# Splitting the input norm's product of x, gain and power into two products, on one core

## The chip, the cores and the metric

The kernel runs on 1 core of one Trainium2 chip. The metric is the device time of one execution in microseconds (us), the median of several runs. Engines are called by their short names: PE (matrix products; PEld is its weight load), DVE (vector), ACT (scalar activations), POOL (GpSimd), SP (the engine whose queue issues the DMAs here).

## The reference

Two layers over x of 256 tokens by 1024 features, float32. Each layer has three sublayers, every one between an input norm and an output norm:

```
def rms_norm(x, g):
    xf = x.astype(jnp.float32)
    y = xf * lax.rsqrt(jnp.mean(xf * xf, axis=-1, keepdims=True) + EPS)
    return (y * g.astype(jnp.float32)).astype(x.dtype)
...
    for l in range(DEPTH):
        h = swiglu(rms_norm(x, ffn1_pre[l]), ffn1_w_gate_up[l], ffn1_w_down[l])
        x = x + 0.5 * rms_norm(h, ffn1_post[l])
        h = hybrid_mixer(rms_norm(x, mix_pre[l]), w_in[l], b_gate[l], conv_w[l],
                         w_conv_out[l], w_pool_group[l], b_pool_group[l],
                         pool_scale[l], w_pool_out[l], w_o[l])
        x = x + rms_norm(h, mix_post[l])
        h = swiglu(rms_norm(x, ffn2_pre[l]), ffn2_w_gate_up[l], ffn2_w_down[l])
        x = x + 0.5 * rms_norm(h, ffn2_post[l])
    return x
```

The mean over features, its power of -0.5 and the gain vector g make the factor; the change concerns `rms_norm` where it stands ahead of a sublayer. There are six of those (two layers of three sublayers).

## The kernel before, in words

Tokens are cut into two blocks of 128 (`NB`, L22), and x stays on the chip as `xs[b]`, 128 tokens by 1024 features. Weights come in chunks of 1 MB through the SP queue; `issue` (L108) loads each in two halves `raw`, ACT copies a rounded high part `hi`, DVE takes the rest `lo`. Every product is made of high and low parts, so PE has three products where the reference has one.

A sublayer ends with `out_product` (L270): it finishes block 0's output first, then calls `on_block(0, ...)` and goes on with the last 12 steps (three matmuls each) of block 1. `on_block` (L524) calls `post` (L216), which adds the normed output to x, and then `pre` (L234), which makes the next sublayer's input `xn`. `turn` (L245) transposes a half of `xn` on PE and splits it into `xt`, which the next sublayer reads. The two halves of block 0 are turned after steps 8 and 10 of those 12 (`TURN0`, L35). Block 1 goes through the same functions after its last step; its halves are turned inside `fill` (L311), the next sublayer's first products, after 5 and 6 half products of block 0 (`TURN1`, L33).

`pre` takes two sums of squares on ACT (`sumsq`, L210, tile `junk`, result `ss`), and then `rstd` (L200): two DVE instructions `v` on one column, the second reading the first's result, and the power `r` on POOL (L207). In block 1 a part of a weight's split (`lo`) stands on DVE between the update of x and `pre` (the `part()` at the end of `post`).

Ahead of the first sublayer the trunk loads x block 0, the gain vector, x block 1 and then weights, all through SP in this order, and runs `pre` and `turn` for block 0; `r` of block 1 is made early, and `pre(1, g0, r)` gets it as an argument. PE has 13 warming matmuls in the meantime.

The order of the instructions on PE, ACT and DVE is the order of the program: `InOrder` (L43) keeps it, and in the profile all these instructions bear its line, L49. The tiles' names tell them apart.

Of the kernel before, what the change touches and what calls it, by code (L numbers as in the profile page):

```python
# [10 lines left out]
F32 = mybir.dt.float32  # L11
# [3 lines left out]
ALU = mybir.AluOpType  # L15

P = 128
T = 256
D = 1024
# [16 lines left out]

# Columns of the per-feature parameters: gate bias, conv taps, pool bias, pool scale.
F_BG, F_CW, F_PB, F_PS, F_N = 0, 16, 40, 48, 56


class InOrder:
    """An engine whose instructions are kept in the order of the program."""

# [9 lines left out]
def trunk(ctx: ExitStack, tc: tile.TileContext, x, gains, feat, wgu1, wd1, win, wco, wpg, wpo, wo, wgu2, wd2, out):  # L53
    nc = tc.nc
# [17 lines left out]

# [1 line left out]
    xs = [const.tile([P, D], F32, name=f"x{b}") for b in range(NB)]  # L74

    def load_x(b):
        for h in HALF:
            nc.sync.dma_start(xs[b][:, h], x[b * P : (b + 1) * P, h])  # L78

    ident = const.tile([P, P], F32, name="ident")  # L80
    make_identity(nc, ident)
    mhalf = const.tile([P, 1], F32, name="mhalf")
    nc.gpsimd.memset(mhalf, -0.5)
    invc = const.tile([P, PAD], F32, name="invc")
    for i in range(PAD):
        nc.gpsimd.memset(invc[:, i : i + 1], 1.0 / (i + 1))

# [1 line left out]
    stream = []  # L89
# [18 lines left out]
    def issue(now=True):  # L108
        """Loads and splits the next chunk, or leaves the parts of the split for part()."""
        i = state["issued"]  # L110
        state["issued"] = i + 1
        name, l, c = stream[i]
        hi = whi.tile([P, CHUNK], F32R, name="hi")
        lo = wlo.tile([P, CHUNK], F32R, name="lo")
        h = CHUNK // 2
        for s in range(2):
            sl = slice(s * h, (s + 1) * h)
            raw = raws.tile([P, h], F32, name="raw")
            nc.sync.dma_start(raw, src[name][l, c, :, sl])
            parts.append(lambda sl=sl, raw=raw: act.copy(hi[:, sl], raw))  # L120
            parts.append(
                lambda sl=sl, raw=raw: dve.tensor_tensor(lo[:, sl], raw, hi[:, sl].bitcast(F32), op=ALU.subtract)
            )
        ready[i] = (hi, lo)
        if now:
            part(4)
# [8 lines left out]
    def chunk(name, held=0):  # L135
        """The next chunk; held: how many of the chunks before it are still to be read."""
        i = state["used"]
        assert stream[i][0] == name, (stream[i], name)
        state["used"] = i + 1
        top_up(held + 1)  # L140
        if state["issued"] == i + 1:
            part(len(parts))
        return ready.pop(i)

    def top_up(held):
        """Loads and splits ahead, into the buffers that are not held; held chunks are still to be
        read. The last split is left to part()."""
        part(len(parts))
        while state["issued"] < min(state["used"] + LOOK + 1 - held, len(stream)):
            part(len(parts))  # L150
            issue(False)

# [1 line left out]
    def split(dst, src_ap, between=0):  # L154
        """dst = (high, low) views; src in PSUM or SBUF, float32."""
        hi, lo = dst
        act.copy(hi, src_ap)
        part(between)
        dve.tensor_tensor(lo, src_ap, hi.bitcast(F32), op=ALU.subtract)

    def feat_product(name, acts_hl):
        """W^T @ act for the two 128-column tiles of a chunk, features on partitions. In each of the
        two banks: the high weights with the high and with the low part of act side by side, and the
        low weights with the high part on top of the first."""
        ps = [bank(), bank()]
        whi_, wlo_ = (t.rearrange("p (k c) -> p k c", c=CC) for t in chunk(name))
        for i in range(2):
            cs = slice(i * P, (i + 1) * P)
            for k in range(KT):
                both, ah, _ = acts_hl[k]  # L170
                pe.matmul(ps[i], whi_[:, k, cs], both, start=(k == 0), stop=False)
                pe.matmul(ps[i][:, :T], wlo_[:, k, cs], ah, start=False, stop=(k == KT - 1))
        return ps

    def add_up(ps, tag, out=None):
        """The two halves of a feature product, added: [128, 2, 256]."""
        t = tmp.tile([P, 2, T], F32, name=tag)
        out = t if out is None else out
        for i in range(2):
            act.copy(t[:, i, :], ps[i][:, T:])  # L180
        part()
        for i in range(2):
            dve.tensor_tensor(out[:, i, :], ps[i][:, :T], t[:, i, :], op=ALU.add)
        return out

    def token_product(o, w, acts_hl, b, ks):
        """o[128 tokens of block b, 256] = act^T @ W chunk."""
        whi_, wlo_ = (t.rearrange("p (k c) -> p k c", c=CC) for t in w)
# [4 lines left out]

# [1 line left out]
    def load_gain(l, which):  # L195
# [4 lines left out]
    def rstd(parts, scale):  # L200
        """(scale * (sum of parts / D + eps)) ** -0.5"""
        v0 = small.tile([P, 1], F32, name="v0")
# [13 lines left out]
    def post(b, banks, gain, scale):  # L216
        """x[b] += rms(h) * gain / sqrt(scale)"""
        u = wide.tile([P, D], F32, name="u")
# [15 lines left out]
    def pre(b, gain, r=None):  # L234
        """rms(x[b]) * gain"""
        if r is None:
            r = rstd([sumsq(xs[b][:, HALF[s]]) for s in range(2)], 1.0)
        xn = wide.tile([P, D], F32, name="xn")
        for s in range(2):
            dve.scalar_tensor_tensor(  # L240
                xn[:, HALF[s]], xs[b][:, HALF[s]], r, gain[s], op0=ALU.mult, op1=ALU.mult
            )
        return xn

    def turn(b, s):  # L245
        """Half of the next sublayer's input of block b, features on partitions, split."""
        xn, xt = state["xn"][b], state["next"][0]
# [11 lines left out]
    def act_slot(dtype=F32):  # L259
        """[128, 2, 512] float32, or twice that in bfloat16"""  # L260
        return acts.tile([P, 2, 512], dtype, name="act", tag="act")

    def split_pair(src_ap):
        """Two feature tiles [128, 2, 256] -> (high and low side by side, high, low) of each"""
        t = act_slot(F32R).rearrange("p i (h t) -> p i h t", h=2)
        split((t[:, :, 0, :], t[:, :, 1, :]), src_ap, 1)
        return [(t[:, i], t[:, i, 0, :], t[:, i, 1, :]) for i in range(2)]

# [1 line left out]
    def out_product(name, nchunk, acts_hl, on_block):  # L270
# [40 lines left out]
    def fill(name, n, turns, acts_hl, take):  # L311
        """n chunks' products, tokens on partitions. Block 0 goes ahead, and after turns[s] halves of
        a product the s-th half of block 1's input is turned. take(b, f, ps) reads the columns of
        one or two chunks, the f-th the last."""
        ws = [chunk(name, LOOK) for _ in range(n)]
# [16 lines left out]

# [1 line left out]
    def turn_back(tok):  # L334
        """[128 tokens, 2, 256 features] of both blocks, as [128 features, 2, 256 tokens] in PSUM."""
        pt = bank()
# [5 lines left out]
    def ffn(l, gu, dn, acts_hl, on_block, nfill, turns, gains_):  # L342
        # The first nfill chunks: gate and up of a pair by turns, and a last gate.
        slot = act_slot()
# [31 lines left out]
    def mixer(l, acts_hl, on_block, nfill, turns, gains_):  # L376
# [3 lines left out]

        # Gates of the conv branch, the first of block 0 ahead of block 1.
        slots = [act_slot() for _ in range(2)]
# [22 lines left out]

        # Gated short convolution.
        ys = []
# [17 lines left out]

        # Pooling over trailing windows.
        ds_ = []
# [21 lines left out]

        # Gates of the pool branch.  # L450
        gp = gates()
# [30 lines left out]

# [1 line left out]
    plan = []  # L484
    for l in range(DEPTH):
        plan += [("ffn", l, "gu1", "d1", 0, 1, 4.0), ("mix", l, None, None, 2, 3, 1.0), ("ffn", l, "gu2", "d2", 4, 5, 4.0)]

    # The tensor engine's clock rises only after some time of work.
    idle = act_slot(BF16)[:, 0, :]
# [54 lines left out]
def _cols(w):  # L544
    """[L, 1024, N] -> [L, N / 256, 128, 8 * 256]: chunks of 256 columns, partitions first."""
    l, k, n = w.shape
# [4 lines left out]
def _rows(w):  # L551
    """[L, K, 1024] -> [L, K / 256, 128, 2 * 1024]: chunks of two row tiles, partitions first."""
    l, k, n = w.shape
# [4 lines left out]
def _gate_up(w):  # L558
    """Chunks of gate columns and of up columns by turns."""
    c = _cols(w)  # L560
# [35 lines left out]
```

## Time and profile before

| | |
|---|---|
| median of 3 runs | 1187.08 us (1185.7 to 1188.16) |
| profiled execution, span from first to last instruction | 1184.7 us |
| PE busy | 1169.6 us (99%) |
| DVE busy | 804.2 us (68%) |
| ACT busy | 639.1 us (54%) |
| POOL busy | 17.2 us (1%) |
| DMA | 225.57 MB, mean 190 GB/s |

For the profiled execution the profile gives the span; a time of its own, with what lies around the span, is not among the numbers shown. Busy time of an engine is the sum of its instructions' times; PE's is modelled, and says where PE had work, not how fast. The rows that bear on the change are below, in groups.

### The profile page before, as it was taken

Reading aid. Unit: us, or ns where it says so; the run is one execution under the profiler, and the core shown is the slowest. Engines: PE = TensorE matmul, PEld = TensorE weight load, DVE = VectorE, ACT = ScalarE, POOL = GpSimd, SP = SyncE. Lnnn points to the kernel's source line nnn. Section 1 sums busy time; section 2 is a strip of 40 time slices with the busy share of each in tenths; the row PEclk is TensorE's granted clock in tenths of the full one; section 3 lists DMA queues with packets and bytes.
Section 4 is the critical chain, followed back from the end, with each engine's and each line's share of the span. In section 5 each row is a group of like instructions: output and inputs, shape, how many; then the busy total and the mean of one; then the engine's idle time right before and its main releaser. Section 6 shows DMA issues by size and latency. Waiting matters only on the chain.

```text
span 1184.7 us, 17127 instructions
## 1 busy us (share of the span) xinstructions
PE 1169.6 (99%) x6625; PEld 1023.1 (86%) x6625; DVE 804.2 (68%) x1092; ACT 639.1 (54%) x997; POOL 17.2 (1%) x75
## 2 busy tenths in 40 slices
PE   7999999999999999999999999999999999999997
PEld 6888888988888898888898888898888888988886
DVE  5776745677987776665476666466789786766742
ACT  5755634655564565554365555356556565655630
POOL 0000000000000000000000000000000000000000
PEclk8999999999999999999999999999999999999999
DMA  7765663655566465667456566536565554756540
GB/s 267 265 188 192 194 228 132 222 184 179 171 202 209 163 230 183 196 190 231 161 193 192 185 195 230 189 128 215 182 204 185 198 181 141 243 184 194 190 167 36
DMA packets 62577, 225.57 MB, mean 190 GB/s; under 512 B 7200, under 2 KB 7200, under 8 KB 62496
## 3 DMA queue, kind: packets, MB, share of 16 engines
q1 hardware_dynamic: 62496, 224.48, 57.5%
q8 instruction: 52, 0.85, 0.3%
q14 instruction: 29, 0.24, 0.1%
HBM read 223.40 MB, written 1.05 MB: 189 GB/s over the span
## 4 chain that ended last, share of the span: by engine, by line
PE 96%; ACT 1%; DVE 1%; DMA 1%; POOL 0%; issue 0%; SPq 0%; DVEq 0%; POOLq 0%; ACTq 0%
PE ps L49 96%; ACT junk L49 1%; DMA x<-in_x 1%; POOL r L207 0%; DVE x L49 0%; DVE xn L49 0%; DVE v L49 0%; DVE lo L49 0%; ACT xt L49 0%; ACT hi L49 0%; SPq L78 0%; DVEq L592 0%; POOLq L592 0%; SPq L197 0%; ACTq L49 0%
## 5 line engine op out<-in xcount | busy, mean ns | idle before, releaser
L49 PE MATMUL ps<-xt,hi 128*128 128x512 f32 x1920 | 667.3, 392 | 0.0
L49 DVE TENSOR_TENSOR lo<-raw,hi 128x1024 fp32r<-128x1024 f32 x412 | 495.0, 1221 | 134.5 <-ACT hi L49 133.5
L49 PE MATMUL ps<-xt,lo 128*128 128x256 f32 x1920 | 537.7, 280 | 0.0
L49 ACT CAST hi<-raw 128x1024 fp32r<-128x1024 f32 x412 | 424.9, 1050 | 103.1 <-PE ps L49 89.1
L49 PEld LDWEIGHTS ps<-xt,hi 128*128 128x128 f32 x1920 | 359.2, 187 | 78.7
L49 PEld LDWEIGHTS ps<-xt,lo 128*128 128x128 f32 x1920 | 362.9, 189 | 0.1
L49 PE MATMUL ps<-hi,act 128*128 128x512 f32 x832 | 260.0, 390 | 0.0
L49 PEld LDWEIGHTS ps<-hi,act 128*128 128x128 f32 x832 | 156.2, 188 | 32.3
L49 PE MATMUL ps<-lo,act 128*128 128x512 f32 x416 | 161.9, 389 | 0.0
L49 ACT COPY h<-ps 128x256 f32<-128x256 f32 x150 | 54.5, 374 | 142.9 <-PE ps L49 141.6
L49 DVE TENSOR_TENSOR h<-ps,h 128x256 f32<-128x256 f32 x150 | 61.6, 420 | 91.7 <-ACT h L49 91.7
L49 ACT COPY sil<-ps 128x256 f32<-128x256 f32 (+1 forms) x126 | 46.7, 374 | 103.5 <-PE ps L49 103.5
L49 PE MATMUL ps<-act,hi 128*128 128x512 f32 (+1 forms) x320 | 102.0, 375 | 0.0
L49 PEld LDWEIGHTS ps<-lo,act 128*128 128x128 f32 x416 | 78.1, 188 | 15.7
L49 PE MATMUL ps<-act,lo 128*128 128x256 f32 x288 | 81.0, 281 | 0.0
L49 DVE TENSOR_TENSOR sil<-ps,sil 128x256 f32<-128x256 f32 x106 | 43.7, 420 | 49.1 <-ACT sil L49 49.1
L49 PE MATMUL ps<-hi,xt 128*128 128x256 f32 x512 | 74.4, 289 | 0.8 <-ACT hi L49 0.8
L49 ACT CAST act<-h 128x512 fp32r<-128x512 f32 x65 | 40.4, 621 | 60.9 <-DVE h L49 60.9
L49 PEld LDWEIGHTS ps<-hi,xt 128*128 128x128 f32 x512 | 67.7, 196 | 1.6 <-ACT hi L49 1.2
L49 PEld LDWEIGHTS ps<-act,hi 128*128 128x128 f32 x320 | 58.1, 189 | 12.0
L49 PEld LDWEIGHTS ps<-act,lo 128*128 128x128 f32 x288 | 54.5, 189 | 0.0
L49 DVE TENSOR_TENSOR act<-h,act 128x512 fp32r<-128x512 f32 (+1 forms) x73 | 50.1, 686 | 6.0 <-ACT act L49 5.7
(57 smaller groups left out, 450.2 us busy)
## 6 DMA issues: line engine op xcount, KB each, us to landing
raw<-in_wgu SPq DMA_DIRECT2D x176, 512.0 KB, 4.6
raw<-in_win SPq DMA_DIRECT2D x96, 512.0 KB, 4.7
raw<-in_wd SPq DMA_DIRECT2D x88, 512.0 KB, 4.6
raw<-in_wco SPq DMA_DIRECT2D x16, 512.0 KB, 5.2
raw<-in_wpo SPq DMA_DIRECT2D x16, 512.0 KB, 4.2
raw<-in_wo SPq DMA_DIRECT2D x16, 512.0 KB, 4.4
gain<-in_gains SPq DMA_DIRECT2D x12, 512.0 KB, 4.6
raw<-in_wpg SPq DMA_DIRECT2D x4, 512.0 KB, 4.2
```

The costliest lines, as they stand in the source:

```text
L49: return lambda *a, **kw: self.tc.keep_in_program_order(f(*a, **kw))
```

## The change

`pre` multiplied x by the power and by the gain in one instruction with three inputs (x, `r` per token, gain). Now it multiplies x by the gain with a `tensor_tensor`, written into `xn`, and afterwards `xn` by `r` in place with a `tensor_scalar`. The first pair of instructions stands in the program behind the sums of squares and ahead of `rstd`. The memset of the constant -0.5 (`mhalf`), which POOL's power reads, moves ahead of the identity matrix. Comments are also gone from the file, which changes line numbers only.

```
+    mhalf = const.tile([P, 1], F32, name="mhalf")
+    nc.gpsimd.memset(mhalf, -0.5)
     ident = const.tile([P, P], F32, name="ident")
     make_identity(nc, ident)
-    mhalf = const.tile([P, 1], F32, name="mhalf")
-    nc.gpsimd.memset(mhalf, -0.5)
...
     def pre(b, gain, r=None):
-        if r is None:
-            r = rstd([sumsq(xs[b][:, HALF[s]]) for s in range(2)], 1.0)
+        ss = [sumsq(xs[b][:, HALF[s]]) for s in range(2)] if r is None else None
         xn = wide.tile([P, D], F32, name="xn")
         for s in range(2):
-            dve.scalar_tensor_tensor(
-                xn[:, HALF[s]], xs[b][:, HALF[s]], r, gain[s], op0=ALU.mult, op1=ALU.mult
-            )
+            dve.tensor_tensor(xn[:, HALF[s]], xs[b][:, HALF[s]], gain[s], op=ALU.mult)
+        if r is None:
+            r = rstd(ss, 1.0)
+        for s in range(2):
+            dve.tensor_scalar(xn[:, HALF[s]], xn[:, HALF[s]], r, None, op0=ALU.mult)
         return xn
```

The order moves on DVE alone; 12 rows come in, and PE, ACT and POOL keep their sequence but for the memset. In the rows below `x_88` is block 0 of x and `x_89` block 1, `x2` means two instructions (the two halves), `v_...` are the one-column steps of `rstd`, and the numbers behind `v` differ between the kernels without meaning.

DVE at the start of the program, before:

```order
L49 TENSOR_SCALAR v_151<-ss 128x1
L49 TENSOR_SCALAR v_153<-ss,v_151 128x1
L49 SCALAR_TENSOR_TENSOR xn<-x_88,r,gain 128x512 x2
L49 TENSOR_SCALAR v_166<-ss 128x1
L49 TENSOR_SCALAR v_168<-ss,v_166 128x1
L49 TENSOR_TENSOR xt<-ps,xt 128x512 x2
L49 TENSOR_TENSOR lo<-raw,hi 128x1024
L49 SCALAR_TENSOR_TENSOR xn<-x_89,r,gain 128x512 x2
```

The same place in the changed kernel:

```order
L49 TENSOR_TENSOR xn<-x_88,gain 128x512 x2
L49 TENSOR_SCALAR v_154<-ss 128x1
L49 TENSOR_SCALAR v_156<-ss,v_154 128x1
L49 TENSOR_SCALAR xn<-xn,r 128x512 x2
L49 TENSOR_SCALAR v_168<-ss 128x1
L49 TENSOR_SCALAR v_170<-ss,v_168 128x1
L49 TENSOR_TENSOR xt<-ps,xt 128x512 x2
L49 TENSOR_TENSOR lo<-raw,hi 128x1024
L49 TENSOR_TENSOR xn<-x_89,gain 128x512 x2
L49 TENSOR_SCALAR xn<-xn,r 128x512 x2
```

For block 0 the products with the gain stand ahead of both `v`, and for block 1 both pairs stand behind the `lo`.

DVE behind the first sublayer's block 0, before:

```order
L49 SCALAR_TENSOR_TENSOR x_88<-u,r,x_88 128x512 x2
L49 TENSOR_SCALAR v_1740<-ss 128x1
L49 TENSOR_SCALAR v_1742<-ss,v_1740 128x1
L49 SCALAR_TENSOR_TENSOR xn<-x_88,r,gain 128x512 x2
L49 TENSOR_TENSOR xt<-ps,xt 128x512
```

In the changed kernel:

```order
L49 SCALAR_TENSOR_TENSOR x_88<-u,r,x_88 128x512 x2
L49 TENSOR_TENSOR xn<-x_88,gain 128x512 x2
L49 TENSOR_SCALAR v_1747<-ss 128x1
L49 TENSOR_SCALAR v_1749<-ss,v_1747 128x1
L49 TENSOR_SCALAR xn<-xn,r 128x512 x2
L49 TENSOR_TENSOR xt<-ps,xt 128x512
```

Two instructions have come between the update of x and the first `v`.

DVE behind the same sublayer's block 1, before:

```order
L49 SCALAR_TENSOR_TENSOR x_89<-u,r,x_89 128x512 x2
L49 TENSOR_TENSOR lo<-raw,hi 128x1024
L49 TENSOR_SCALAR v_1832<-ss 128x1
L49 TENSOR_SCALAR v_1834<-ss,v_1832 128x1
L49 SCALAR_TENSOR_TENSOR xn<-x_89,r,gain 128x512 x2
```

In the changed kernel:

```order
L49 SCALAR_TENSOR_TENSOR x_89<-u,r,x_89 128x512 x2
L49 TENSOR_TENSOR lo<-raw,hi 128x1024
L49 TENSOR_TENSOR xn<-x_89,gain 128x512 x2
L49 TENSOR_SCALAR v_1841<-ss 128x1
L49 TENSOR_SCALAR v_1843<-ss,v_1841 128x1
L49 TENSOR_SCALAR xn<-xn,r 128x512 x2
```

Here the two come behind a `lo`, again ahead of both `v`. Block 0 and block 1 have these rows after five sublayers; after the last there is no `pre`.

## Rows read from the trace of the kernel before

**Rows 1.** The page: the span, and the share of each engine.

```profile
span 1184.7 us, 17127 instructions
PE 1169.6 (99%) x6625; PEld 1023.1 (86%) x6625; DVE 804.2 (68%) x1092; ACT 639.1 (54%) x997; POOL 17.2 (1%) x75
```

**Rows 2.** Waits of PE: us in total, times, longest.

```profile
PE ps L49 <- DVE xn L49: 6.2, 6, 4.0
```

**Rows 3.** Timeline, the start: start us, us, engine, line, op, out<-in, [idle before <-releaser].

```profile
9.20 1.41 DVE L49 SCALAR_TENSOR_TENSOR xn<-x,r,gain 128x512 f32<-128x512 f32 x2 [3.81 <-DMA gain<-in_gains]
10.01 1.97 PE L49 MATMUL ps<-ident,xn 128*128 128x128 f32 x8 [3.98 <-DVE xn L49]
10.59 0.63 ACT L49 ACTIVATE junk<-x 128x512 bf16<-128x512 f32 x1
11.22 0.57 ACT L49 CAST xt<-ps 128x512 fp32r<-128x512 f32 x1
...
15.00 1.41 DVE L49 SCALAR_TENSOR_TENSOR xn<-x,r,gain 128x512 f32<-128x512 f32 x2
...
15.14 1.22 PE L49 MATMUL ps<-lo,xt 128*128 128x256 f32 x4 [0.27 <-DVE lo L49]
...
16.16 1.05 PE L49 MATMUL ps<-ident,xn 128*128 128x128 f32 x4
...
17.25 0.59 ACT L49 CAST xt<-ps 128x512 fp32r<-128x512 f32 x1 [3.08 <-PE ps L49]
```

**Rows 4.** Timeline behind the first sublayer, block 0.

```profile
193.12 1.42 DVE L49 SCALAR_TENSOR_TENSOR x<-u,r,x 128x512 f32<-128x512 f32 x2
...
195.48 0.21 DVE L49 TENSOR_SCALAR v<-ss,v 128x1 f32<-128x1 f32 x1 [0.60 <-ACT junk L49]
...
196.36 1.42 DVE L49 SCALAR_TENSOR_TENSOR xn<-x,r,gain 128x512 f32<-128x512 f32 x2 [0.66 <-POOL r L207]
...
197.25 0.63 PE L49 MATMUL ps<-ident,xn 128*128 128x128 f32 x4 [0.39 <-DVE xn L49]
```

**Rows 5.** Timeline behind the first sublayer, block 1.

```profile
205.50 0.14 DVE L49 TENSOR_SCALAR v<-ss 128x1 f32<-128x1 f32 x1
205.75 0.22 DVE L49 TENSOR_SCALAR v<-ss,v 128x1 f32<-128x1 f32 x1
...
206.69 1.41 DVE L49 SCALAR_TENSOR_TENSOR xn<-x,r,gain 128x512 f32<-128x512 f32 x2 [0.73 <-POOL r L207]
...
208.14 0.60 PE L49 MATMUL ps<-ident,xn 128*128 128x128 f32 x4
```

**Rows 6.** Timeline, block 1 behind the third and the fifth sublayer.

```profile
603.35 1.41 DVE L49 SCALAR_TENSOR_TENSOR xn<-x,r,gain 128x512 f32<-128x512 f32 x2 [0.73 <-POOL r L207]
...
604.45 0.60 PE L49 MATMUL ps<-ident,xn 128*128 128x128 f32 x4
...
999.17 1.42 DVE L49 SCALAR_TENSOR_TENSOR xn<-x,r,gain 128x512 f32<-128x512 f32 x2 [0.66 <-POOL r L207]
...
1000.75 0.60 PE L49 MATMUL ps<-ident,xn 128*128 128x128 f32 x4
```

**Rows 7.** DVE by form: op, out<-in, xcount | busy us, mean ns of one | idle before.

```profile
L49 DVE SCALAR_TENSOR_TENSOR xn<-x,r,gain 128x512 f32<-128x512 f32 x24 | 17.0, 748 | 10.7 <-POOL r L207 6.9 <-DMA gain<-in_gains 3.8
L49 DVE SCALAR_TENSOR_TENSOR h<-cu,ft,h 128x256 f32<-128x256 f32 x32 | 14.8, 484 | 5.7 <-ACT h L49 5.2
L49 DVE TENSOR_SCALAR v<-ss,v 128x1 f32<-128x1 f32 x24 | 5.1, 214 | 27.6 <-ACT junk L49 26.5
```

**Rows 8.** Timeline of DVE: a product of two tiles in SBUF, and what follows it.

```profile
302.02 0.68 DVE L49 TENSOR_TENSOR act<-h,act 128x512 fp32r<-128x512 f32 x1
302.62 1.22 DVE L49 TENSOR_TENSOR lo<-raw,hi 128x1024 fp32r<-128x1024 f32 x1
```

**Rows 9.** Stretches: us, PE busy, granted clock of PE (1.00 is 2.4 GHz), DMA share, GB/s.

```profile
10.00:18.00 8.00, 6.91 (x29) 0.50 0.76 287
...
18.70:19.00 0.30, 0.30 (x5) 1.00 1.06 437
```

## The prediction

> **What bounds the kernel now.** The page comes first: PE is busy for 1169.6 of 1184.7 us, DVE for 68% of the span [rows 1]. So time on DVE as such costs nothing, and only what makes PE wait does. The second view is the list of PE's waits. Its largest row is the wait for `xn`, the very tile that the change concerns: 6.2 us in six places, the longest 4.0 us at the start [rows 2]. The other five are one behind each of the first five sublayers, where the first half of block 0 is turned; the first is 0.39 us long [rows 4]. Block 1's `xn` never stops PE: it comes a little ahead of its transposes [rows 5, 6]. The third view is the timeline at these places, which gives the distances between instructions. Because PE has no other idle time behind the start, whatever delays it at one place is still there at the end. The kernel is bound by PE, and the change by how much later or earlier `xn` reaches it.
>
> **The prices.** The removed instruction, one with three inputs, costs 748 ns [rows 7]. A product of two tiles of 128x512 in SBUF lets the next DVE instruction start 0.60 us later (302.02 to 302.62) [rows 8], so the new pair with the gain holds DVE for 1.20 us. The new scaling by `r` has no row: no instruction of this kernel reads one wide float32 tile in SBUF and a column. Call its time d. From below it is bound by the same operation on one column, 214 ns, from above by the removed instruction, which has the same column operand, the same elements and one tile more, 748 ns [rows 7]. I take the middle, d = 0.48, and keep both ends. One row speaks for it: the three-input instruction with half the elements takes 484 ns [rows 7], and the scaling would cost about that if, with one tile to read in place of two, it took two elements at a time.
>
> The nearest row in shape is the one of 748 ns, and by it the sum below is 8.7 us. The Trainium skill says otherwise (VectorE: DVE Perf Modes, section "Mode 2×_2P — use both read ports for one tensor"): an operation with a single source streams two float32 elements at a time when source and destination are in SBUF, while `tensor_tensor` cannot. By that rule 256 element times would go from the upper end, which leaves an estimated 0.48 us for d and 5.5 us for the sum. No row of this trace has the case, so it can neither bear the rule out nor refute it.
>
> **Block 0 behind a sublayer, five times.** The words of the change suggest that the product with the gain lies under the power on POOL. In the order on DVE it stands ahead of both `v`, and POOL's power waits for the second `v`. So it lies under ACT's sums of squares, and holds up the `v` if it lasts longer than they do. The update of x starts at 193.12; two of its instructions take 1.42, so they start 1.42 - 0.75 = 0.67 apart, and the products can begin at 193.12 + 2 x 0.67 = 194.46. They hold DVE to 195.66. The first `v` starts then, the second 0.25 later (the distance in [rows 5]), at 195.91 instead of 195.48 [rows 4]. The sums are done sooner than that, so DVE's queue decides: `r` is 0.43 late. The scaling then saves 0.75 - d. With d = 0.48 the first half of `xn` is 0.43 - 0.27 = 0.16 late. PE is already waiting for it (0.39 us [rows 4]), so all of it shows: 5 x (d - 0.32) = **0.8 us**. The second half is turned two steps later, and is covered.
>
> **Block 1 behind a sublayer, five times.** Before, the `v` follow at once on the `lo` [rows 5], so the products push them and `r` by their full 1.20 us. The first half of `xn` is 1.20 - 0.75 + d = 0.93 late. Against that stands the lead it had. Taking from [rows 4] that PE starts 0.14 us behind the end of the first half (197.25 - 196.36 - 0.75), PE could have started in the first place at 206.69 + 0.75 + 0.14 = 207.58 and did at 208.14, a lead of 0.56 [rows 5]. By the same working it is 0.21 behind the third sublayer and 0.69 behind the fifth [rows 6]; behind the second and fourth the rows read like the first, 0.58 and 0.55. The leads add up to 2.59. New waits: 5 x 0.93 - 2.59 = 5d - 0.34 = **2.1 us**.
>
> **The start.** The three-input instruction waited here for the gain's DMA until 9.20, with `r` ready long before (the releaser in [rows 3] is the DMA). Now the first product waits for it, and behind it stand the `v` and the power that used to be done by then. From 9.20: 1.20 for the pair, 0.25 to the second `v`, 0.88 from there to the instruction that reads `r` (195.48 to 196.36 [rows 4]): the scaling starts at 11.53 and ends at 12.01, where the old one ended at 9.95. PE's transposes start 2.06 later. ACT's first cast stood behind a sum of squares that ended at 11.22 (10.59 + 0.63); from the transposes alone it could have started at 10.01 + 1.09 = 11.10 (1.09 is the same step at 16.16 to 17.25 [rows 3]). So 0.12 of the delay is covered and 1.94 = 1.46 + d goes on through ACT's and DVE's queues to the first products. Next is block 1: its `r` is there, but both pairs stand behind the first `lo` and the transposes wait for 0.93 more, with a lead of 16.16 - 15.00 - 0.75 - 0.14 = 0.27 [rows 3]; the new wait is 0.18 + d = 0.66. Together **2.6 us**. The next `lo` comes later too, by what PE itself has been delayed and 0.2 more; the transposes and matmuls between cover that.
>
> The clock counts here. It was granted at 0.50 from 10 to 18 us and at 1.00 from 18.7 [rows 9], after PE had worked without a pause since 15.14 [rows 3]. If it rises as much later as the work does, nothing is added, and I take 0. If it rises at the same moment, 2.6 us of work runs at the full clock and half, 1.3 us, comes back. If the new pause ahead of 16.16 puts it off, another 1.0 us of work (15.14 to 16.16) stays at the low one, at a cost of 0.5.
>
> **What costs nothing.** The memset moved on POOL: its constant is first read microseconds later. DVE's 24 extra instructions of some 0.6 us lie in its 32% of idle time, but for the places above; without that cover they would cost 24 x 0.6 = 14 us. A `lo` behind `pre` frees its DMA buffer up to a microsecond later; PE waits for no weights behind the start. The last sublayer has no `pre`, so the tail stays.
>
> **The sum** is 1.64 + 2d at the start, 5d - 1.60 and 5d - 0.34 behind the sublayers: 12d - 0.30. With d = 0.48 that is 5.5 us, with 0.21 it is 2.2, with 0.75 it is 8.7. On the span of 1184.7 us it makes 1190.2. The median of the runs is 2.4 us above the span, which is what lies around it and the difference between runs (they lie 2.5 us apart); I keep it as it is: 1187.1 + 5.5 = **1192.6 us**.
>
> **The rivals.**
> - *The scaling costs as much as what it replaces* (d = 0.75). For it: the nearest row in shape. Against it: one tile less to read. 1187.1 + 8.7 = 1195.8.
> - *Not slower: the scaling is nearly free of its length.* At every place the path of `xn` trades a late `r` for a shorter last step. With d under 0.22 the sum is under 2.4 us, which is 0.2% and about what a measurement of this kernel can tell from no change. That gives 1189.3 or less. For it: the one-column row of 214 ns. Against it: every wide row of DVE grows with its elements (484 to 748 ns).
> - *The products do stay beside the power, as the words of the change have it.* If DVE's queue let the `v` go ahead, each block 0 would gain 0.27 (1.35 in five, less than PE waits there), block 1 would lose nothing, and the start would lose only 1.20 - 0.27 - 0.12 = 0.8: 1186.5. Against it: the order on DVE, which is kept.
>
> **How the numbers follow.** Forecast, d between 0.35 and 0.6: 0.66. Full price: 0.20. Nearly free: 0.07. Beside the power: 0.05. The last 0.02 is for a gain by something unseen. The range runs from 1189.0 (short d, or the forecast with the clock rising early and a lower base) to 1196.0 (full price). Slower by over 0.2% takes the first two, 0.86; no change the next two, 0.12; faster 0.02.
>
> **What would show it.** In the changed kernel the first transposes should start near 12.1 us and the clock should rise near 21 us; PE's wait for `xn` should grow from six places to about twelve, from 6.2 us to some 6.2 + 2.1 + 0.7 + 0.8 + 2.1 = 12; behind block 0 the second `v` should start 2.8 us behind the update of x instead of 2.4, with DVE no longer idle ahead of it. The row of `xn<-xn,r` gives d and with it the sum. I am wrong if the `v` start when they did before, if block 1's transposes still wait for nothing, or if delays of PE at the start are made up behind it.

## The result, and the profile after

The changed kernel takes 1195.56 us in the median of 6 runs (1193.04 to 1199.78), the kernel before 1186.65 (1185.7 to 1188.16, 6 runs): a ratio of 1.0077 with a 95% interval of 1.0065 to 1.0089. It is slower, by 8.9 us where 5.5 were forecast. The profiled execution took 1196.88 us, more than the median, so its trace holds somewhat more than the usual loss.

The page and PE's waits of the changed kernel, beside [rows 1, 2]:

```profile
span 1195.1 us, 17150 instructions
PE 1177.2 (98%) x6625; PEld 1024.4 (86%) x6625; DVE 811.8 (68%) x1116; ACT 639.4 (54%) x997; POOL 17.2 (1%) x75
...
PE ps L49 <- DVE xn L49: 8.9, 9, 5.2
```

The span has grown by 10.4 us, but PE waits for `xn` only 2.7 us longer, and its busy time has grown by 7.6 us (1169.6 to 1177.2) with the same 6625 matmuls. So waits cannot be the whole story. First the part that was looked for. The start, beside [rows 3]:

```profile
8.05 1.29 DVE L49 TENSOR_TENSOR xn<-x,gain 128x512 f32<-128x512 f32 x2 [6.92 <-DMA gain<-in_gains]
...
9.52 0.21 DVE L49 TENSOR_SCALAR v<-ss,v 128x1 f32<-128x1 f32 x1
...
10.40 0.88 DVE L49 TENSOR_SCALAR xn<-xn,r 128x512 f32<-128x512 f32 x2 [0.67 <-POOL r L207]
10.94 1.97 PE L49 MATMUL ps<-ident,xn 128*128 128x128 f32 x8 [5.21 <-DVE xn L49]
...
17.09 0.87 DVE L49 TENSOR_SCALAR xn<-xn,r 128x512 f32<-128x512 f32 x2
17.62 1.11 PE L49 MATMUL ps<-ident,xn 128*128 128x128 f32 x4 [0.38 <-DVE xn L49]
```

The gain landed 1.15 us sooner than in the trace of before (8.05 against 9.20). Measured from there, PE's first transposes come after 2.89 us instead of 0.81: 2.08 later, and block 1's transposes wait for `xn` where they waited for nothing. Behind the first sublayer, beside [rows 4], and block 1, beside [rows 5]:

```profile
197.28 1.41 DVE L49 SCALAR_TENSOR_TENSOR x<-u,r,x 128x512 f32<-128x512 f32 x2
...
198.61 1.29 DVE L49 TENSOR_TENSOR xn<-x,gain 128x512 f32<-128x512 f32 x2
...
199.82 0.15 DVE L49 TENSOR_SCALAR v<-ss 128x1 f32<-128x1 f32 x1
200.07 0.21 DVE L49 TENSOR_SCALAR v<-ss,v 128x1 f32<-128x1 f32 x1
...
200.95 0.88 DVE L49 TENSOR_SCALAR xn<-xn,r 128x512 f32<-128x512 f32 x2 [0.66 <-POOL r L207]
201.58 0.63 PE L49 MATMUL ps<-ident,xn 128*128 128x128 f32 x4 [0.56 <-DVE xn L49]
...
211.03 0.15 DVE L49 TENSOR_SCALAR v<-ss 128x1 f32<-128x1 f32 x1
...
212.22 0.88 DVE L49 TENSOR_SCALAR xn<-xn,r 128x512 f32<-128x512 f32 x2 [0.73 <-POOL r L207]
212.76 0.66 PE L49 MATMUL ps<-ident,xn 128*128 128x128 f32 x4 [0.15 <-DVE xn L49]
```

The second `v` starts 2.79 us behind the update of x (200.07 - 197.28) where it was 2.36, with no idle time of DVE ahead of it, and PE waits 0.56 for block 0 instead of 0.39. Block 1's transposes now wait. The one price that was bracketed (the tile's own view: ns of one, smallest, median, largest):

```profile
L49 DVE TENSOR_SCALAR xn<-xn,r x24: 477/481/488, 10.4 to 1009.0; 128x512 f32<-128x512 f32 x24
```

Compare the start times of the same matmul in the two traces, place by place. PE loses 2.1 us up to 25 us, 0.15 to 0.17 where block 0 is turned behind each of the five sublayers (0.8 together), and 0.37, 0.24, 0.38, 0.36 and 0.23 at the five places of block 1 (1.6). That is 4.5 of the 10.4. The view of waits shows only a part of this (0.15 at the first place of block 1, where the starts show 0.37 lost), and it counts from the ends of matmuls, which are modelled. The rest comes where nobody waits. Here are six stretches of 60 us, one in the long feature products of each sublayer (us, PE busy with its matmuls counted, granted clock, DMA share, GB/s). First one stretch of the kernel before, whose six count 347 to 349, then the changed kernel:

```profile
450.00:510.00 60.00, 60.00 (x348) 1.00 0.60 191
```

```profile
60.00:120.00 60.00, 60.00 (x341) 1.00 0.59 187
250.00:310.00 60.00, 60.00 (x348) 1.00 0.60 194
450.00:510.00 60.00, 60.00 (x341) 1.00 0.60 188
640.00:700.00 60.00, 60.00 (x348) 1.00 0.60 187
830.00:890.00 60.00, 60.00 (x348) 1.00 0.56 184
1040.00:1100.00 60.00, 60.00 (x341) 1.00 0.59 184
```

PE is busy throughout at the full clock, yet in three sublayers it starts 341 matmuls where it started 348. From start to start these are 176.6 us for 1000 matmuls instead of 173.3. In each case the slower pace lasts for some 600 matmuls, about 2.0 us, and the three make 6.0. They begin behind a group of transposes in which PE multiplies by the identity matrix (`turn_back`), and end with the feature products. So the open question was what sets this pace: the split, or the other edit of the diff.

### The profile page after: what moved, and what is told of

It is laid out like the page before. It is cut to its first block, busy times and chain, and to the rows that moved or that the text cites. A ratio compares the mean times of both kernels' runs of the same rounds, so it can differ in the third digit from the quotient of the medians.

```text
span 1195.1 us, 17150 instructions
## 1 busy us (share of the span) xinstructions
PE 1177.2 (98%) x6625; PEld 1024.4 (86%) x6625; DVE 811.8 (68%) x1116; ACT 639.4 (54%) x997; POOL 17.2 (1%) x75
## 4 chain that ended last, share of the span: by engine, by line
PE 93%; DVE 4%; ACT 1%; POOL 1%; issue 1%; DMA 1%; DVEq 0%; SPq 0%; POOLq 0%; ACTq 0%
PE ps L49 93%; DVE xn L49 1%; DVE x L49 1%; POOL r L207 1%; DVE lo L49 1%; DMA gain<-in_gains 1%; DVE v L49 0%; ACT junk L49 0%; ACT hi L49 0%; ACT xt L49 0%; DVE xt L49 0%; DVE u L49 0%; SPq L78 0%; DVEq L593 0%; POOLq L593 0%
```

## The experiments

Three theories stood against each other. **P**: the split of the product does all of it, also the slower pace, by the times at which PE now waits. **A**: the waits cost some 4 us, and the rest comes from where the identity matrix lies. In the built program the tile of the constant -0.5, allocated first, pushes it from byte 24704 of each partition to 24736; no other tile that PE reads has moved. **M**: the order of POOL's first instructions does it.

**The constant alone** (`e1_memset_moved`), on the kernel before:

```
+    mhalf = const.tile([P, 1], F32, name="mhalf")
+    nc.gpsimd.memset(mhalf, -0.5)
     ident = const.tile([P, P], F32, name="ident")
     make_identity(nc, ident)
-    mhalf = const.tile([P, 1], F32, name="mhalf")
-    nc.gpsimd.memset(mhalf, -0.5)
```

> The kernel before, with one edit: the constant -0.5 is allocated and set ahead of the identity matrix, as in the changed kernel. The product of x, r and gain is left as before. In the built program this moves the identity matrix by 32 bytes in SBUF, from 24704 to 24736, and no other tile that PE reads. Theory A (the address): PE has two paces in the long stretches of feature products, 173.3 and 176.6 us per 1000 matmuls; the trace of the changed kernel shows the slower one in three of six sublayers, at some 2.0 us each, always from the group of transposes with the identity matrix onwards. If the identity's place sets it, this kernel takes about 1191 us (1.5 to 8 us more than before), with the slower pace in one to four sublayers and PE's waits for xn as before (6.2 us). Theory P (the products): the slower pace follows from the later xn; then this kernel takes what before takes, 1186.6, within 0.1%.

Measured: 1190.23 us against 1187.14, ratio 1.0030 (1.0018 to 1.0041). This is what theory A says. The stretches of this kernel, whose instructions are those of before:

```profile
60.00:120.00 60.00, 60.00 (x341) 1.00 0.58 189
250.00:310.00 60.00, 60.00 (x341) 1.00 0.56 189
450.00:510.00 60.00, 60.00 (x348) 1.00 0.58 190
...
830.00:890.00 60.00, 60.00 (x342) 1.00 0.58 193
```

It has three slow stretches again, partly in other sublayers (both mixers), while `xn` comes as before. The slower pace needs no late `xn`. The trace is that of the slowest of six executions (1192.63; the fastest took 1187.85), so others may well have had fewer slow stretches: only profiled executions show them.

**The split alone** (`e2_split_only`): the changed kernel with those four lines put back.

> The changed kernel with the constant -0.5 put back behind the identity matrix: the split product alone. Theory A (the address): only the waits are left, 0.8 us behind block 0 and 1.3 us behind block 1 as in the changed kernel's trace, and 2.1 at the start: 4.2 us over before, some 1190.8 us, with no stretch at the slower pace behind the transposes. Theory P (the products): 1195.6 us, as the changed kernel, with the slower pace in some of the sublayers.

Measured: 1192.31 us, ratio 1.0050 (1.0038 to 1.0063): 5.2 us, nearer to A than to P, though the interval leaves out both totals (A had counted block 1 at the first transposes alone, 1.3 instead of 1.6, and the start at 2.1). The stretches decide it. They are these, with PE's wait:

```profile
60.00:120.00 60.00, 60.00 (x348) 1.00 0.59 192
250.00:310.00 60.00, 60.00 (x348) 1.00 0.57 191
450.00:510.00 60.00, 60.00 (x348) 1.00 0.58 188
...
PE ps L49 <- DVE xn L49: 10.1, 9, 6.0
```

None of the six is slow; the other three count 348 and 349. The places lose 0.83 us at block 0 and 1.91 at block 1 (0.37, 0.24, 0.71, 0.35, 0.24), by the same matching of starts. The two edits add up: 3.1 + 5.2 = 8.3 of the 8.9.

**Place or order** (`e3_tile_order`, `e4_memset_order`): the tile allocated first with its memset behind, and the memset first with its tile behind.

```
+    mhalf = const.tile([P, 1], F32, name="mhalf")
     ident = const.tile([P, P], F32, name="ident")
     make_identity(nc, ident)
-    mhalf = const.tile([P, 1], F32, name="mhalf")
     nc.gpsimd.memset(mhalf, -0.5)
```

> The kernel before; the constant's tile is allocated ahead of the identity matrix (identity at 24736), but its memset stays behind the identity's, so that POOL has the order of before. Theory A (the address): as with the constant moved whole, 1.5 to 8 us more than before, about 1191. Theory M (the order of POOL's first instructions): no change, 1186.6. Theory P: no change.

```
     ident = const.tile([P, P], F32, name="ident")
-    make_identity(nc, ident)
     mhalf = const.tile([P, 1], F32, name="mhalf")
     nc.gpsimd.memset(mhalf, -0.5)
+    make_identity(nc, ident)
```

> The kernel before; all tiles at their places (identity at 24704), but POOL sets the constant -0.5 ahead of the identity matrix. Theory A (the address): no change, 1186.6 within 0.1%. Theory M (the order of POOL's first instructions): 1.5 to 8 us more. Theory P: no change.

Measured: 1190.74 (1.0033, 1.0021 to 1.0045) for the place, 1187.77 (1.0004, 0.9996 to 1.0013) for the order. M falls. P falls too, since the place alone costs 3.6 us with no split product. With the place changed both mixers are slow, and the other four stretches count 347 to 349:

```profile
250.00:310.00 60.00, 60.00 (x341) 1.00 0.53 179
...
830.00:890.00 60.00, 60.00 (x342) 1.00 0.56 192
```

One thing did not fit: with the identity at its old place the first sublayer counted 341 in `e4_memset_order`; the other five counted 347 to 349.

**Another place** (`e5_ident_64`):

```
+    invc = const.tile([P, PAD], F32, name="invc")
     ident = const.tile([P, P], F32, name="ident")
...
-    invc = const.tile([P, PAD], F32, name="invc")
```

> The kernel before; the table of reciprocals (64 bytes) is allocated ahead of the identity matrix, which so moves by 64 bytes, from 24704 to 24768, where a move by 32 bytes cost 3.1 to 3.6 us. No instruction changes. If the step within 64 bytes is what counts: no change, 1187.1 within 0.1%, and the fast pace in sublayers 2 to 6. If any other place than the one of before costs: about 1190.5.

Measured: 1191.49, ratio 1.0042 (1.0029 to 1.0056). 64 bytes further is no better than 32; both mixers and the first sublayer count 342. The mixers:

```profile
250.00:310.00 60.00, 60.00 (x342) 1.00 0.56 186
...
830.00:890.00 60.00, 60.00 (x342) 1.00 0.57 190
```

That left two readings: the old place was good by accident, or it is good as a multiple of 128 bytes (24704 is 193 x 128, the two others are not).

**A place that is a multiple of 128** (`e9_ident_128` on the kernel before, `e10_changed_ident_128` on the changed one): the identity at 16512.

```
+    ident = const.tile([P, P], F32, name="ident")
     xs = [const.tile([P, D], F32, name=f"x{b}") for b in range(NB)]
...
-    ident = const.tile([P, P], F32, name="ident")
```

> The kernel before; the identity matrix is allocated ahead of x, at 16512 instead of 24704. Both are multiples of 128 bytes, while the two places that cost time, 24736 and 24768, are not. x moves by 512 bytes, the rest stays. Theory of the 128-byte step: no change, 1187.3 within 0.1%, and the fast pace in the long stretch of sublayers 2 to 6, as at 24704. Theory that the place of before is good by accident: some 1190 to 1191.5, as at the two other places.

> The changed kernel with one edit: the identity matrix is allocated ahead of x, at 16512. POOL's constant stays ahead of the identity's memset, as changed. Theory of the 128-byte step: only the waits of the split product are left, about 1192.3 as with the constant put back. Theory of the accident: 1195.6 as the changed kernel.

Measured: 1187.56 against 1186.89 (1.0005, 0.9994 to 1.0016), and 1191.40 (1.0044, 1.0030 to 1.0058). Both agree with the step of 128 bytes, and the stretches of both kernels count 347 to 349 in all six sublayers. Two of the three that were slow in the changed kernel, now in `e10_changed_ident_128`:

```profile
450.00:510.00 60.00, 60.00 (x347) 1.00 0.57 188
...
1040.00:1100.00 60.00, 60.00 (x348) 1.00 0.59 191
```

So where these tiles lie decides about half of the changed kernel's loss. Two things remain open. The two good places lie 8192 bytes apart, so good places that recur every 256 or 512 bytes, and so on up to 8192, fit them as well as every 128: shown are two places that cost nothing and two that cost time, not the rule. And the constant -0.5 was back at its old byte, 25216, in both of these kernels, while in all four kernels with a costly place it lay elsewhere (24704, or 25280 in `e5_ident_64`). PE never reads the constant, and the slower pace begins behind products that read the identity matrix, so the identity matrix is the likelier cause; but no run put it at a costly place with the constant left at 25216.

**The start** (`e8_start_as_before`): in `pre`, the split only behind sublayers.

```
+        split_ = r is None and "xn" in state
+        if split_:
+            for s in range(2):
+                dve.tensor_tensor(xn[:, HALF[s]], xs[b][:, HALF[s]], gain[s], op=ALU.mult)
...
         for s in range(2):
+            if split_:
+                dve.tensor_scalar(xn[:, HALF[s]], xn[:, HALF[s]], r, None, op0=ALU.mult)
+            else:
                 dve.scalar_tensor_tensor(
```

> The split product behind the five sublayers, with the constant at its old place; at the start of the program both blocks keep the one instruction of before. This tells the start's share from the share behind the sublayers. By the sum of the prediction, with the measured leads: 0.8 us for block 0 and 1.9 for block 1, 2.7 together, so about 1189.8, and the start would hold the other 2.5 of the 5.2 us that the split alone cost. If the start costs nothing because the clock rises earlier: 1192.3, as the split alone.

Measured: 1189.49 against 1187.28, ratio 1.0020 (1.0011 to 1.0029): 2.2 us behind the sublayers, and so about 5.2 - 2.2 = 3.0 at the start, where 2.7 and 2.5 were expected. Both medians have an interval of more than a microsecond either way, so the difference is rough.

**The product beside the power** (`e6_v_first`): `rstd` called ahead of the first pair, as the words of the change have it, on the kernel before with the constant at its place.

```
         if r is None:
             r = rstd([sumsq(xs[b][:, HALF[s]]) for s in range(2)], 1.0)
...
+            dve.tensor_tensor(xn[:, HALF[s]], xs[b][:, HALF[s]], gain[s], op=ALU.mult)
+        for s in range(2):
+            dve.tensor_scalar(xn[:, HALF[s]], xn[:, HALF[s]], r, None, op0=ALU.mult)
```

> The split product with the constant at its old place, and the product with the gain behind the second v, so that it stands beside the power on POOL, as the words of the change have it. Queue theory (only DVE's order counts): behind block 0 the scaling starts 1.33 us behind the second v and ends at 1.81, where the old instruction's first half ended at 1.63: 0.18 later, five times, 0.9 us; block 1 is late by the same 0.18, less than its leads of 0.21 to 0.69, and costs nothing; the start costs 1.0 for block 0 and 0.66 for block 1. Sum 2.6: about 1189.7, and POOL's power starts 0.3 us behind the second v as before. Port theory (POOL's power cannot read while DVE reads two tiles in SBUF): the power starts some 1.3 us behind the second v, and the sum is about 7: 1194. The Trainium skill states such a lock (SBUF — State Buffer, section on who interferes with whom); by it the second would come true.

Measured: 1189.27, ratio 1.0021 (1.0011 to 1.0032), as the queue theory has it. Its timeline behind the first sublayer, block 0:

```profile
197.42 0.21 DVE L49 TENSOR_SCALAR v<-ss,v 128x1 f32<-128x1 f32 x1 [0.60 <-ACT junk L49]
197.55 1.28 DVE L49 TENSOR_TENSOR xn<-x,gain 128x512 f32<-128x512 f32 x2
197.71 0.93 POOL L207 TENSOR_TENSOR r<-v,mhalf 128x1 f32<-128x1 f32 x1 [2.69 <-DVE v L49]
198.75 0.88 DVE L49 TENSOR_SCALAR xn<-xn,r 128x512 f32<-128x512 f32 x2
```

The scaling starts 1.33 behind the second `v`, as reckoned from the queue, with DVE not idle ahead of it. The power does suffer, with 0.93 us instead of 0.55 (0.86 to 0.93 at the ten such places), but it starts at its usual time and ends ahead of the second product, so that the delay is covered. The Trainium skill (SBUF — State Buffer, "Who interferes with whom") states an exclusive lock between a DVE instruction with two inputs in SBUF and one of POOL that reads SBUF: the later of the two blocks for the whole of the first. The trace shows a delay, and a shorter one: the first product takes 0.68 us and had 0.52 left when the power started, and the power lost 0.38. The port theory had reckoned with one lock over both products, 1.28 us, and that did not come. Even truly beside the power the split product is slower than one instruction.

**Half of it, at the place where PE waits** (`e7_half_ahead`): only the first half of block 0, with its product in the time of ACT's sums; all else as before.

```
+        ahead = r is None and xs[b] is xs[0] and "xn" in state
...
+            if ahead:
+                dve.tensor_tensor(xn[:, HALF[0]], xs[b][:, HALF[0]], gain[0], op=ALU.mult)
+            r = rstd(ss, 1.0)
+        if ahead:
+            dve.tensor_scalar(xn[:, HALF[0]], xn[:, HALF[0]], r, None, op0=ALU.mult)
+        for s in range(1 if ahead else 0, 2):
             dve.scalar_tensor_tensor(
```

> The kernel before, constant at its old place; only the first half of block 0's input, behind the five sublayers, is split: its product with the gain (0.6 us on DVE) stands between the update of x and the first v, in the time in which DVE waits for ACT's second sum of squares, and the scaling (0.48 us) follows the power. The second half, block 1 and the start stay as before. If the account of the waits is right, the product costs nothing there, since the second v still starts when ACT's sum is done, and the first half of xn is 0.75 - 0.48 = 0.27 us earlier at five places where PE waits 0.39 to 0.52: 1.35 us less, about 1185.8, with PE's waits at these places at 0.12 to 0.25. If the scaling's start is bound otherwise: no change, 1187.1.

Measured: 1185.53 against 1187.28, ratio 0.9992 (0.9983 to 1.0001), which settles nothing alone. Its timeline behind the first sublayer:

```profile
194.34 1.42 DVE L49 SCALAR_TENSOR_TENSOR x<-u,r,x 128x512 f32<-128x512 f32 x2
...
195.67 0.69 DVE L49 TENSOR_TENSOR xn<-x,gain 128x512 f32<-128x512 f32 x1
...
196.69 0.21 DVE L49 TENSOR_SCALAR v<-ss,v 128x1 f32<-128x1 f32 x1 [0.28 <-ACT junk L49]
...
197.57 0.49 DVE L49 TENSOR_SCALAR xn<-xn,r 128x512 f32<-128x512 f32 x1 [0.66 <-POOL r L207]
197.97 0.75 DVE L49 SCALAR_TENSOR_TENSOR xn<-x,r,gain 128x512 f32<-128x512 f32 x1
198.21 0.63 PE L49 MATMUL ps<-ident,xn 128*128 128x128 f32 x4
```

The second `v` starts 2.35 behind the update of x, as in [rows 4], and PE's transposes 3.87 behind it instead of 4.13. Matched against before, each of the five places gains 0.26 to 0.28. The same kernel was run once more:

> The kernel in which only block 0's first half is split, a second time, to narrow its interval: 1.35 us less than before by the account of the waits, about 1185.9; 1187.3 if the first result (0.9992) was chance.

Measured: 1184.88 against 1186.89, ratio 0.9987 (0.9978 to 0.9995). This version beats the kernel before by some 0.1%, and so the changed one too. In this trace the five places gain 0.24 to 0.28 each, so that they account for the 0.1% in both.

## Why the prediction was right, and where its size was off

- *What bounds the kernel.* Right: delays of PE at the start and behind the sublayers are all still there at the end.
- *The scaling, d = 0.48 between 0.21 and 0.75.* It took 0.481 us. The rule of the Trainium skill that was weighed there (VectorE: DVE Perf Modes, "Mode 2×_2P — use both read ports for one tensor") agrees with this trace, and the nearest row in shape was the wrong guide.
- *Block 0, 0.8 us.* Measured 0.8 in the changed kernel and in the split alone; the second `v` came 0.43 later, as worked out.
- *Block 1, 2.1 us.* 1.6 in the changed kernel, 1.9 in the split alone. They differ at one place, behind the third sublayer (0.38 and 0.71), where the lead was forecast as the shortest.
- *The start, 2.6 us.* PE's transposes came 2.08 behind their old distance from the gain (forecast 2.06). What the whole start costs is known less well: 3.0 by the medians. By the starts of the same matmul at 25 us, the three traces with the changed order at the start (the changed kernel, `e2_split_only`, `e10_changed_ident_128`) are 2.1, 1.3 and 1.6 behind the trace of before, and the other eight with the old order 0.2 to 1.4 ahead of it: 2.4 in the mean. The clock of the changed kernel in its profiled execution:

```profile
10.00:18.00 8.00, 5.64 (x22) 0.50 0.67 258
...
18.70:21.00 2.30, 2.30 (x13) 0.50 0.97 328
21.60:22.00 0.40, 0.40 (x6) 1.00 1.49 317
```

  Full clock came between 21 and 21.6 us instead of 18.7 [rows 9], as forecast ("near 21 us"), but this was luck. With the same order on DVE at the start full clock was granted by 18.2 us in `e2_split_only` and by 19.9 in `e10_changed_ident_128`:

```profile
18.20:18.50 0.30, 0.17 (x2) 1.00 0.86 341
...
19.90:20.50 0.60, 0.60 (x7) 1.00 1.03 348
```

  The nine traces with the old order have it from 16.0 (`e5_ident_64`) to 18.7 us, the one of before the latest. So a single trace does not tell what the change does to the clock, and the choice between the three cases of the prediction stays open.
- *The sum.* 5.5 us was forecast for the split, and the split alone cost 5.2.
- *The sign of PE's waits, about twelve and 12 us.* The view shows nine and 8.9 in the changed kernel. At the start the gain landed 1.15 us sooner, and at block 1 the view shows only a part of what PE lost.
- *"What costs nothing. The memset moved on POOL: its constant is first read microseconds later."* This is the step that failed. As an instruction the memset did cost nothing (1.0004). Its tile came with it, took the identity matrix's place and moved that by 32 bytes, and this alone cost 3.1 us (3.6 and 4.2 in the two other kernels before with the identity matrix off its place). The prediction looked at what the lines issue and not at what they allocate. That the median (1195.56) stayed within the range (up to 1196.0) was luck: its upper end had been drawn for another reason, the full price of the scaling.
- *The rivals.* The full price and the nearly free scaling both fell with the row of 481 ns. The product beside the power was in fact not what the change does; where the order is made so, it costs 0.2% instead of gaining, since the two products put the scaling 1.33 us behind the second `v`, where the power alone put it at 0.88.

## What to carry to other kernels

Splitting a three-input instruction to use another engine's waiting time paid here only on the half that is waited for, and can pay only if the added piece ends before the instruction that it is put ahead of could have started anyway. When lines that allocate are moved, compare the tiles' places in the built program before costing the edit at nothing. If PE's busy time grows with the same matmuls, count them in equal stretches before looking for waits.

## What the runs showed that had not been expected

- PE has two paces in the same stream of matmuls at the same clock, 348 and 341 starts in 60 us, and keeps one for some 600 matmuls. At the faster pace two distances from start to start alternate, 117 and 230 ns; at the slower one six repeat, 118, 241, 120, 236, 113 and 232. In the sublayers two to six the long stretch was at the faster pace in all 45 cases (nine executions of eight kernels) with the identity at a multiple of 128 bytes; with it 32 or 64 bytes off, it was at the slower one in two of five sublayers in each of the four kernels.
- The first sublayer follows no such rule: it was slow in three of those nine as well (`e4_memset_order`, `e7_half_ahead`, `e8_start_as_before`), and fast in `e11_half_ahead_again`, which is the same kernel as `e7_half_ahead`. So its pace differs between executions of one kernel, by 2.1 us, and of the three slow stretches of the changed kernel the first cannot be put down to the identity's place. What decides there stays open, and so does why the identity's place acts on matmuls that do not read it; that the transposes choose the pace is read from where it begins, and was not tried by itself.
- A power of one column on POOL took 0.86 to 0.93 us instead of 0.55 while DVE read two tiles in SBUF.
